# Per-head scale-and-add on VectorE in a gMLP and dilated-attention trunk: the merge of attention groups 0 and 1, and the output tiles

## The chip, the cores and the metric

The kernel runs on one core of a Trainium2 chip. The metric is the device time of one launch in microseconds (us). Names of engines: PE is TensorE, DVE is VectorE, ACT is ScalarE, POOL is GpSimd, SP is SyncE, which issues all the DMAs here.

## The reference

A trunk of two layers works on 2048 tokens of width 1024, all in float32. The first layer is a gated MLP with causal mixing inside chunks of 128 tokens. The second is attention in three groups of eight query heads of 128 columns each, with dilations 1, 4 and 16, over one shared K/V. What the change touches is how the three groups' results become one:

```
m = jnp.max(sc, axis=-1, keepdims=True)
p = jnp.exp(sc - m)
l = jnp.sum(p, axis=-1, keepdims=True)
...
lse = jnp.moveaxis((m + jnp.log(l))[..., 0], -1, 3)
...
alpha = jax.nn.softmax(jnp.stack(lses), axis=0)
o = jnp.sum(alpha[..., None] * jnp.stack(outs), axis=0).astype(x.dtype)
y = o.reshape(bsz, s, B_WIDTH) * jax.nn.silu(z)
return x + gate * (y @ w_out)
```

So for each token and head, three vectors of 128 columns are added with three weights, which differ by token and by head; the sum is multiplied by silu(z) and goes into the last matrix product.

## The kernel before

The tokens are worked through in four quarters of 512. For each quarter `layer_A` makes the gated MLP (products `v`, `u`, `z`, `o`), and `proj_B` makes K/V, the queries and z of the second layer. Every matrix is split into a high and a low part (`split`, lines 247 and 248: ACT copies the high part, DVE subtracts the low part), and a product is three passes on PE. The weights stream through a pool of 8 split buffers (`wp`) and 6 raw ones (`rp`).

Attention is a generator, `attend`, whose steps are called as side work ("fillers") between the matmuls of the main products by `tick`. A unit is one group `g`, one block `b` of 128 queries and one K/V head `kh` (four query heads). `att_1` transposes K and Q, `att_2` makes scores, maxima and exponentials (line 1103 on DVE adds distance times slope to the scores, line 1113 on ACT takes the exponentials), `att_3` transposes the probabilities (line 1155) and `att_4` multiplies them with V into the PSUM tile `po` (line 1174) and evacuates that into `ot`, which a DMA stores. Group 1 of quarter Q is worked off, and then group 0, beside `layer_A` of quarter Q + 1. The last quarter has no next one: its group 1 and group 0 run beside the output product.

**The merge of groups 0 and 1** sits in `att_3` and `att_4` for g = 0. `att_3` makes the factor `e1` for four heads (line 1134, ACT) and loads group 1's stored result `o1` (line 1136, a tile named `st_o`). `att_4` scales `o1` by `e1` on POOL (`scale_heads`, line 1225, one instruction over 128x512 with the factor broadcast along each head), updates the sums of weights on DVE with two instructions on 128x4 (lines 1169 and 1170), and adds `po` and the scaled `o1` on DVE (line 1178). There are 32 such units, 8 for each quarter.

**The output tiles** are in `finish`. For each of 16 tiles of 128 tokens, `load(t)` brings the merged result of groups 0 and 1 (`og[0]`), that of group 2 (`og[2]`) and z; `prepare(t)` scales `og[0]` by eight ACT instructions, one for each head (line 1287), scales `og[2]` on DVE (`scale_heads`, line 1225, 128x1024), adds the two on DVE (line 1289) and multiplies with z on POOL (line 1290). `make_yb(t)` transposes the result on PE (line 1312) and splits it (lines 1314 and 1315), and lines 1352 to 1354 are the output product `pf`, 48 matmuls for each tile, followed by line 1357 (DVE, gate), line 1358 (POOL, plus x) and a store. Tiles are prepared two ahead of the product. Tile 0 is prepared inside the last projection (`z3b`), tiles 1 to 11 beside group 1 of the last quarter, and the four tiles that need the last quarter's merge after it.

The order on each engine is not the order of the code alone: a scheduling pass sorts the instructions of all engines by its own costs, and each engine then works its list strictly in order. So an instruction that waits holds up everything behind it on its engine.

## Time and profile before

| | us |
|---|---|
| median of 3 runs | 2974.0 (2972.69 to 2979.12) |
| the profiled execution | 2975.72, of which its span is 2973.7 |
| PE busy | 2922.2 (98%) |
| DVE busy | 2114.8 (71%) |
| ACT busy | 1652.1 (56%) |
| POOL busy | 751.2 (25%) |

The page of the profile gives each engine's busy time, the span in 40 slices, and groups of instructions by line, each with its count, its busy time, the mean duration, and the idle time of its engine just ahead of it with the one that ended that idle time. The trace can also be asked for the busy times in a stretch of the span, for who waited for whom, and for single instructions in order of time. A busy PE is not PE at its peak, since the matmuls overlap: 512 columns are recorded as some 0.39 us, and the next one starts 0.23 us after.

### The profile page before, as it was taken

Reading aid. Unit: us, or ns where it says so; the run is one execution under the profiler, and the core shown is the slowest. Engines: PE = TensorE matmul, PEld = TensorE weight load, DVE = VectorE, ACT = ScalarE, POOL = GpSimd, SP = SyncE. Lnnn points to the kernel's source line nnn. Section 1 sums busy time; section 2 is a strip of 40 time slices with the busy share of each in tenths; the row PEclk is TensorE's granted clock in tenths of the full one; section 3 lists DMA queues with packets and bytes.
Section 4 is the critical chain, followed back from the end, with each engine's and each line's share of the span. In section 5 each row is a group of like instructions: output and inputs, shape, how many; then the busy total and the mean of one; then the engine's idle time right before and its main releaser. Section 6 shows DMA issues by size and latency. Waiting matters only on the chain. (4 is left out here: it accounts for less than half of the span.)

```text
span 2973.7 us, 45555 instructions
## 1 busy us (share of the span) xinstructions
PE 2922.2 (98%) x14752; PEld 2446.6 (82%) x14752; DVE 2114.8 (71%) x3794; ACT 1652.1 (56%) x3386; POOL 751.2 (25%) x1044
## 2 busy tenths in 40 slices
PE   7999999999999999999999999999999999999999
PEld 5888788878888888888888888888888888977887
DVE  6877676788556676877758676877668667878772
ACT  4323355766565365776546366675555457867440
POOL 1057002320002313502315214403314220122322
PEclk9999999999999999999999999999999999999999
DMA  8899975886344466884334466873333476788642
GB/s 280 275 306 341 310 237 179 261 301 203 123 125 125 131 196 203 280 271 128 110 115 132 139 196 210 298 243 107 115 117 122 137 228 193 230 285 289 221 162 92
DMA packets 368450, 596.08 MB, mean 200 GB/s; under 512 B 39018, under 2 KB 138572, under 8 KB 368212
## 3 DMA queue, kind: packets, MB, share of 16 engines
q1 hardware_dynamic: 368212, 593.17, 61.8%
q8 instruction: 117, 1.92, 0.3%
q14 instruction: 121, 0.99, 0.1%
HBM read 472.84 MB, written 120.20 MB: 199 GB/s over the span
## 5 line engine op out<-in xcount | busy, mean ns | idle before, releaser
L276 PE MATMUL pd_o<-w_o,yh 128*128 128x512 f32 x1024 | 324.8, 397 | 3.0 <-DVE w_o L248 3.0
L276 PE MATMUL pd_kv<-w_kv,hkh 128*128 128x512 f32 x768 | 239.3, 393 | 0.3
L276 PEld LDWEIGHTS pd_o<-w_o,yh 128*128 128x128 f32 x1024 | 187.7, 189 | 40.8 <-DVE w_o L248 4.2
L314 PE MATMUL pd_u<-hAh,w_u 128*128 128x512 f32 x512 | 208.0, 406 | 0.0
L314 PE MATMUL pd_z<-hAh,w_z 128*128 128x512 f32 x512 | 203.8, 398 | 0.0
L276 PE MATMUL pd_o<-w_o,yl 128*128 128x512 f32 x512 | 200.9, 393 | 0.0
L316 PE MATMUL pd_u<-hAh,w_u 128*128 128x512 f32 x512 | 200.6, 392 | 0.0
L316 PE MATMUL pd_z<-hAh,w_z 128*128 128x512 f32 x512 | 200.1, 391 | 0.0
L315 PE MATMUL pd_u<-hAl,w_u 128*128 128x512 f32 x512 | 199.7, 390 | 0.0
L315 PE MATMUL pd_z<-hAl,w_z 128*128 128x512 f32 x512 | 199.4, 389 | 0.0
L247 ACT ACTIVATE w_u<-raw_u 128x512 fp32r<-128x512 f32 x128 | 79.8, 629 | 166.9 <-PE pd_u L316 93.0
L247 ACT ACTIVATE w_z<-raw_z 128x512 fp32r<-128x512 f32 x128 | 80.3, 631 | 160.0 <-PE pd_z L316 74.5
L276 PEld LDWEIGHTS pd_kv<-w_kv,hkh 128*128 128x128 f32 x768 | 143.2, 189 | 30.7 <-ACT hkh L566 2.0
L248 DVE TENSOR_TENSOR w_z<-raw_z,w_z 128x512 fp32r<-128x512 f32 x128 | 108.2, 853 | 80.9 <-ACT w_z L247 80.4
L1174 PEld LDWEIGHTS po<-kv,pT 128*128 128x128 f32 x1200 | 148.1, 191 | 9.1 <-ACT pT L1019 2.2
L1174 PE MATMUL po<-kv,pT 128*128 128x128 f32 x1200 | 150.6, 275 | 1.2 <-ACT pT L1019 1.2
L247 ACT ACTIVATE w_o<-raw_o 128x512 fp32r<-128x512 f32 x128 | 79.4, 628 | 129.9 <-PE pd_o L276 92.2
L276 PE MATMUL pd_kv<-w_kv,hkl 128*128 128x512 f32 x384 | 149.5, 391 | 0.0
L1113 ACT ACTIVATE pr<-pr,stat,rt 128x256 f32<-128x256 f32 (+1 forms) x224 | 123.0, 551 | 31.1 <-DVE stat L1107 15.5
L248 DVE TENSOR_TENSOR w_o<-raw_o,w_o 128x512 fp32r<-128x512 f32 x128 | 94.7, 749 | 39.5 <-ACT w_o L247 38.2
L248 DVE TENSOR_TENSOR w_u<-raw_u,w_u 128x512 fp32r<-128x512 f32 x128 | 94.0, 749 | 34.0 <-ACT w_u L247 32.1
L248 DVE TENSOR_TENSOR w_q<-raw_q,w_q 128x512 fp32r<-128x512 f32 x144 | 96.9, 693 | 24.0 <-ACT w_q L247 22.9
(826 smaller groups left out, 8030.3 us busy)
## 6 DMA issues: line engine op xcount, KB each, us to landing
raw_q<-in_b_w_in_dram SPq DMA_DIRECT2D x144, 256.0 KB, 3.6
raw_u<-in_a_w_in_dram SPq DMA_DIRECT2D x128, 256.0 KB, 3.7
raw_z<-in_a_w_in_dram SPq DMA_DIRECT2D x128, 256.0 KB, 2.9
raw_o<-in_a_w_out_dram SPq DMA_DIRECT2D x128, 256.0 KB, 3.1
qt<-qd SPq DMA_DIRECT2D x96, 260.0 KB, 3.1
raw_v<-in_a_w_in_dram SPq DMA_DIRECT2D x96, 256.0 KB, 4.2
raw_kv<-in_w_kv_dram SPq DMA_DIRECT2D x96, 256.0 KB, 2.9
od<-ot SPq DMA_DIRECT2D x96, 256.0 KB, 2.7
```

The lines of the kernel that those rows point to most:

```text
L247: nc.scalar.activation(hi, src, AF.Copy)
L248: nc.vector.tensor_tensor(lo, src, hi.bitcast(F32), ALU.subtract)
L276: last_mm[0] = nc.tensor.matmul(pt, a, u[:, w, :], start=f, stop=e, skip_group_check=more)
L314: nc.tensor.matmul(pts[i], wh, hh[:, k, :], start=k == 0, stop=False)
L315: nc.tensor.matmul(pts[i], wh, hl[:, k, :], start=False, stop=False)
L316: nc.tensor.matmul(pts[i], wl, hh[:, k, :], start=False, stop=k == KT - 1)
L1113: nc.scalar.activation(pr[:, i, :], pr[:, i, :], AF.Exp, bias=mneg[:, i:i + 1], scale=u["rt"][:, h:h + 1], accum_out=lsum[:, i:i + 1])
L1174: nc.tensor.matmul(po[:, h * P:(h + 1) * P], u["pT"][h // hp][:, h % hp, j, :], u["kv"][:, j, kh, 1, :], start=j == 0, stop=j == nk - 1)
```

## The change

Two places change, and the helper `scale_heads` goes.

```
-            scale_heads(nc.gpsimd, u["o1"], u["o1"], e1)
             nc.vector.tensor_tensor(l1, l1, e1, ALU.mult)
             nc.vector.tensor_tensor(l0, l0, l1, ALU.add)
...
         if g == 0:
-            nc.vector.tensor_tensor(ot, po, u["o1"], ALU.add)
+            for h in range(4):
+                hs = slice(h * P, (h + 1) * P)
+                nc.vector.scalar_tensor_tensor(ot[:, hs], u["o1"][:, hs], stat[1][:, b, kh * 4 + h:kh * 4 + h + 1],
+                                               po[:, hs], ALU.mult, ALU.add)
...
-            scale_heads(nc.vector, og[2], og[2], st2[:, t, 0:8])
-            nc.vector.tensor_tensor(y, y, og[2], ALU.add)
+            for h in range(8):
+                hs = slice(h * P, (h + 1) * P)
+                nc.vector.scalar_tensor_tensor(y[:, hs], og[2][:, hs], st2[:, t, h:h + 1], y[:, hs],
+                                               ALU.mult, ALU.add)
```

In the merge, one POOL instruction and one DVE instruction on 128x512 become four DVE instructions on 128x128, each of which takes a head of `o1` times its factor plus that head of `po`. In an output tile, two DVE instructions on 128x1024 become eight on 128x128. The bytes moved by DMA and the matmuls stay what they were, in number and shape.

The scheduling pass gives other lists. PE's list is unchanged up to the start of the output product; from there on some steps of attention stand up to three `pf` matmuls earlier (the first one of the transposes `pp1_12_00` comes after 37 of them, where it came after 40). Three places show what moves elsewhere. The names carry group, block and head: `ot0_9_0` is group 0, block 9, K/V head 0; in `og6_0` and `og6_2` the first number is the tile and the second the group.

DVE in the merge of a middle quarter (group 0, block 9), before and then in the change; `w_o30_...` are split weights of the main product, `stat0` and `stat1` the sums:

```order
L248 TENSOR_TENSOR w_o30_1_1_21842<-raw_o30_1_1_21843,w_o30_1_1_21842 128x512
L1178 TENSOR_TENSOR ot0_9_0_21730<-po0_9_0_21721,st_o19_0_21613 128x512
L1070 COPY rt0_11_1_21996<-qt0_11_1_21817 128x8
L1169 TENSOR_TENSOR stat1_194<-stat1_194 128x4
L1170 TENSOR_TENSOR stat0_193<-stat0_193,stat1_194 128x4
L248 TENSOR_TENSOR w_o30_1_2_21847<-raw_o30_1_2_21848,w_o30_1_2_21847 128x512
```

```order
L248 TENSOR_TENSOR w_o30_1_1_21880<-raw_o30_1_1_21881,w_o30_1_1_21880 128x512
L1179 TENSOR_SCALAR ot0_9_0_21765<-st_o19_0_21649,stat1_194,po0_9_0_21756 128x128 x4
L1168 TENSOR_TENSOR stat1_194<-stat1_194 128x4
L1169 TENSOR_TENSOR stat0_193<-stat0_193,stat1_194 128x4
L248 TENSOR_TENSOR w_o30_1_2_21885<-raw_o30_1_2_21886,w_o30_1_2_21885 128x512
```

The four new instructions stand where the one stood; only a small copy has moved out from between.

DVE beside group 1 of the last quarter, where tile 6 is prepared, before and then in the change:

```order
L1225 TENSOR_TENSOR og6_2_27046<-og6_2_27046,wst_192 128x1024
L1106 TENSOR_REDUCE rt1_14_0_26743<-pr1_14_01_26840 128x2
L1066 TENSOR_SCALAR qT1_14_1_26869<-pq1_14_1_26864,gqk_481,qT1_14_1_26869 128x512
L1107 TENSOR_SCALAR stat1_194<-rt1_14_0_26743 128x2
L1017 COPY ot1_13_1_26886<-po1_13_1_26877 128x512
L1357 TENSOR_TENSOR of1_1_26892<-pf1_1_26754,gb1_25848 128x512
L1070 COPY rt1_15_1_27095<-qt1_15_1_26953 128x8
L1289 TENSOR_TENSOR og6_0_27044<-og6_0_27044,og6_2_27046 128x1024
L1017 COPY pT1_14_01_26914<-pp1_14_01_26909 128x512
```

```order
L1286 TENSOR_SCALAR og6_0_27122<-og6_2_27124,wst_192,og6_0_27122 128x128
L1106 TENSOR_REDUCE rt1_14_0_26809<-pr1_14_01_26912 128x2
L1066 TENSOR_SCALAR qT1_14_1_26941<-pq1_14_1_26936,gqk_481,qT1_14_1_26941 128x512
L1107 TENSOR_SCALAR stat1_194<-rt1_14_0_26809 128x2
L1286 TENSOR_SCALAR og6_0_27122<-og6_2_27124,wst_192,og6_0_27122 128x128 x3
L1017 COPY ot1_13_1_26958<-po1_13_1_26949 128x512
L1286 TENSOR_SCALAR og6_0_27122<-og6_2_27124,wst_192,og6_0_27122 128x128
L1355 TENSOR_TENSOR of1_1_26964<-pf1_1_26820,gb1_25896 128x512
L1070 COPY rt1_15_1_27173<-qt1_15_1_27025 128x8
L1286 TENSOR_SCALAR og6_0_27122<-og6_2_27124,wst_192,og6_0_27122 128x128 x3
L1017 COPY pT1_14_01_26986<-pp1_14_01_26981 128x512
```

The two long instructions become eight short ones, spread between the same steps of attention.

The last place is where group 0 of the last quarter begins, at block 12 beside output tile 5. ACT before, and then in the change:

```order
L1287 ACTIVATE og10_0_27992<-og10_0_27992,stat0_193 128x128 x7
L1287 ACTIVATE og11_0_28257<-og11_0_28257,stat0_193 128x128 x7
L1055 ACTIVATE kT0_12_27337<-pk0_12_27332 128x512
L1065 ACTIVATE qT0_12_0_27345<-pq0_12_0_27340,gqk_481 128x512
L1287 ACTIVATE og11_0_28257<-og11_0_28257,stat0_193 128x128
L1314 ACTIVATE yb5_27393<-pyb5_0_27394 128x512
```

```order
L1283 ACTIVATE og10_0_28102<-og10_0_28102,stat0_193 128x128 x8
L1055 ACTIVATE kT0_12_27421<-pk0_12_27416 128x512
L1065 ACTIVATE qT0_12_0_27429<-pq0_12_0_27424,gqk_481 128x512
L1312 ACTIVATE yb5_27477<-pyb5_0_27478 128x512
L1312 ACTIVATE yb5_27477<-pyb5_1_27485 128x512
L1283 ACTIVATE og11_0_28379<-og11_0_28379,stat0_193 128x128 x3
L1113 ACTIVATE pr0_12_00_27441,stat0_193<-pr0_12_00_27441,stat0_193,rt0_12_0_27432 128x256 x2
```

Seven scalings of tile 11 stood ahead of the two copies `kT0_12` and `qT0_12_0`; now none does, and three of them stand ahead of the exponentials `pr0_12_00`.

SP at the same place, before and then in the change:

```order
L1280 DMA zt10_27996<-zd_101 128x1024
L1278 DMA og11_0_28257<-od0_95 128x1024
L1339 DMA xr14_0_27303<-x1d_90 128x512
L1359 DMA out_0_dram<-of3_1_27299 128x512
L1136 DMA st_o112_1_27562<-od1_96 128x512
```

```order
L1357 DMA out_0_dram<-of3_1_27383 128x512
L1136 DMA st_o113_1_27903<-od1_96 128x512
L1136 DMA st_o114_0_28008<-od1_96 128x512
L1136 DMA st_o114_1_28159<-od1_96 128x512
L1136 DMA st_o115_0_28259<-od1_96 128x512
L1039 DMA qt0_13_0_27524<-qd0_92 128x520
L1274 DMA og11_0_28379<-od0_95 128x1024
L1357 DMA out_0_dram<-of4_0_27470 128x512
```

The load of tile 11 (`og11_0`) has moved from ahead of the store `of3_1` to behind the load of the queries `qt0_13_0`.

More of the change, by code (lines that the diff above doesn't have):

```diff
@@ L1219, in attend @@
                     yield
-    def scale_heads(e, out, t, f):
-        n = f.shape[-1]
-        e.tensor_tensor(out.rearrange("p (h d) -> p h d", d=P), t.rearrange("p (h d) -> p h d", d=P),
-                        f.unsqueeze(2).broadcast_to([P, n, P]), ALU.mult)
     sw = wst.rearrange("p (a g) (t c) -> p a (g t) c", a=4, c=16)
```

## The prediction

> **What bounds the kernel now.** First I read the span and the busy times of the engines, then the busy times by stage for the stages that the change touches.

> ```profile
> span 2973.7 us, 45555 instructions
> PE 2922.2 (98%) x14752; PEld 2446.6 (82%) x14752; DVE 2114.8 (71%) x3794; ACT 1652.1 (56%) x3386; POOL 751.2 (25%) x1044
> ```

> ```profile
> 905.00:1035.00 130.00, 129.35 (x699) 110.00 (x699) 94.32 (x203) 62.50 (x143) 43.59 (x56) 1.00 0.43 134
> 1560.00:1690.00 130.00, 130.00 (x708) 111.16 (x707) 95.26 (x204) 65.30 (x142) 56.78 (x72) 1.00 0.42 130
> 2205.00:2335.00 130.00, 130.00 (x712) 111.18 (x711) 101.53 (x216) 68.02 (x146) 56.90 (x72) 1.00 0.42 129
> 2690.00:2800.00 110.00, 101.55 (x633) 88.08 (x632) 85.39 (x152) 70.36 (x196) 37.96 (x19) 0.98 0.82 278
> 2800.00:2880.00 80.00, 79.92 (x517) 70.44 (x516) 67.78 (x155) 38.66 (x113) 20.96 (x17) 1.00 0.42 137
> ```

> Columns: the stage, its length, then busy us of PE, weight loads, DVE, ACT and POOL, the granted PE clock, DMA share and GB/s. The first three rows hold 24 of the 32 merges, the fifth the last 8. In these four PE stands still for 0.65, 0, 0 and 0.08 us. The fourth row, group 1 of the last quarter with ten output tiles, is the only stage touched that has idle PE time to speak of: 110 − 101.55 = 8.45 us.

> So I looked for who ends PE's idle time in the fourth stage, in the PE rows of the timeline (the four that the change can reach); the bracket has the idle time and its releaser.

> ```profile
> 2705.52 0.44 PE L1155 MATMUL pp<-ident,pr 128*128 128x128 f32 x2 [1.44 <-ACT pr L1113]
> 2742.51 0.44 PE L1155 MATMUL pp<-ident,pr 128*128 128x128 f32 x2 [1.21 <-ACT pr L1113]
> 2763.70 1.02 PE L1155 MATMUL pp<-ident,pr 128*128 128x128 f32 x4 [1.19 <-ACT pr L1113]
> 2793.18 0.58 PE L1098 MATMUL ps<-kT,qT 128*128 128x256 f32 x1 [2.90 <-ACT qT L1065]
> ```

> Three waits are for the exponentials of a unit (together 3.84 us), one of 2.90 us is for a copy of transposed queries. Nearly everything else is PE's own time.

> **The merges.** Removed per unit: one POOL scaling and one DVE add. Added: four DVE instructions on 128x128.

> ```profile
> L1225 POOL TENSOR_TENSOR st_o<-st_o,stat x32: 1032/1042/1530, 925.1 to 2866.7; 128x512 f32<-128x512 f32 x32
> L1178 DVE TENSOR_TENSOR ot<-po,st_o 128x512 f32<-128x512 f32 x32 | 21.9, 684 | 13.2 <-PE po L1174 12.9 <-DMA raw_o<-in_a_w_out_dram 0.2
> L1103 DVE SCALAR_TENSOR_TENSOR b_s<-dist,rt,ps 128x128 f32<-128x128 f32 x64 | 18.0, 343 | 3.3 <-PE ps L1094 3.3
> ```

> The third row is the new instruction's twin: the same operation, 128x128, one operand in SBUF, one in PSUM, a factor per partition, 343 ns. Four are 4 x 343 = 1372 ns against 684, so DVE gets 688 ns more per unit: the fused form is not less DVE work, it pays a start four times. [...]

> Against it stands something that the removed POOL instruction does to DVE:

> ```profile
> L1169 DVE TENSOR_TENSOR stat<-stat 128x4 f32<-128x4 f32 x32 | 10.6, 332 | 6.2 <-ACT stat L1134 6.2
> L1170 DVE TENSOR_TENSOR stat<-stat,stat x32: 145/388/1228, 919.2 to 2867.8; 128x4 f32<-128x4 f32 x32
> L1170 DVE TENSOR_TENSOR stat<-stat,stat 128x4 f32<-128x4 f32 x32 | 15.6, 487 | 0.7
> L1169 DVE TENSOR_TENSOR stat<-stat x32: 145/164/996, 919.0 to 2866.8; 128x4 f32<-128x4 f32 x32
> ```

> Two instructions on 128x4 that can run in 145 to 164 ns take 332 and 487 ns on average and up to 1228, about the length of a POOL scaling that starts on the same event. If all of that excess is POOL holding DVE up, a unit gets back (332 − 164) + (487 − 164) = 491 ns. So DVE's net is between +197 and +688 ns per unit, at most 8 x 688 = 5.5 us in a stage of 130 us in which DVE is idle for 28 us or more (101.53 of 130 in the fullest). On the path that costs nothing as long as PE is fed ahead:

> ```profile
> L247 ACT ACTIVATE w_o<-raw_o 128x512 fp32r<-128x512 f32 x128 | 79.4, 628 | 129.9 <-PE pd_o L276 92.2
> ```

> ACT, the first of the two that split weights, waits 92 us for PE to free a buffer; DVE follows ACT. Weights are ready up to 8 buffers ahead, so 0.7 us in a DVE queue is absorbed. If that cover failed, the 24 units of the first three stages could cost 24 x 0.688 = 16.5 us at the very most; idle PE time of 0 to 0.65 us says they don't. I take **0** for all 32 merges, with 0 to +2 us in the range.

> **The output tiles.** Removed per tile: two DVE instructions. Added: eight. Both operands lie in SBUF, for which the trace has no 128x128 row; the nearest is 128x512.

> ```profile
> L1225 DVE TENSOR_TENSOR og<-og,wst x16: 1210/1220/3086, 2650.3 to 2893.4; 128x1024 f32<-128x1024 f32 x16
> L1289 DVE TENSOR_TENSOR og<-og,og x16: 1212/1220/2570, 2654.1 to 2895.6; 128x1024 f32<-128x1024 f32 x16
> L709 DVE SCALAR_TENSOR_TENSOR acc_a<-aw,sc,acc_a 128x512 f32<-128x512 f32 x28 | 21.0, 751 | 0.8
> L838 DVE SCALAR_TENSOR_TENSOR mt<-pm,colsb,b_s 128x512 f32<-128x512 f32 x64 | 47.4, 744 | 11.0 <-PE pm L836 10.2
> ```

> At 512 columns the operation takes 751 ns from SBUF and 744 with one operand in PSUM, so I take the 343 ns again: 8 x 343 = 2744 ns against 1220 + 1220 = 2440, **+0.30 us a tile**. The ends: a quarter of 751 is 188 ns each, which makes −0.94 us a tile; and one full hold-up by POOL in each tile, of the length that the longest row shows (3086 − 1220 = 1.87 us), makes +2.17. For the ten tiles of the fourth stage that is +3.0 us of DVE (−9.4 to +21.7) where DVE is idle for 110 − 85.4 = 24.6 us. What of it is on the path: the three waits for exponentials are units without cover, and DVE's scores and maxima stand ahead of the exponentials. At about a tile a unit I charge each wait 0.30 us, so +0.9, and 0.2 for the first, whose transposes come three matmuls (0.7 us) earlier while its scores come two earlier (0.5 us). **+1.1 us.** The eight pieces let an urgent step pass sooner than a piece of 1.22 us did; that would cut into the same three waits, and is priced among the rivals. Tile 0, in the last projection, ends within half a microsecond of where it did, since its last add waits for ACT either way: 0. The six tiles left lie beside a PE that is idle for 0.08 us: 0.

> **The wait of 2.90 us.** This is where the new lists matter most.

> ```profile
> 2698.53 0.28 PE L1098 MATMUL ps<-kT,qT 128*128 128x256 f32 x1
> 2698.65 0.28 PE L1099 MATMUL ps<-kT,qT 128*128 128x256 f32 x1
> ...
> 2783.41 0.32 SPq L1278 DMA_DIRECT2D og<-od  x1
> 2784.02 0.39 PE L1353 MATMUL pf<-wo,yb 128*128 128x512 f32 x1
> 2784.24 0.39 PE L1354 MATMUL pf<-wo,yb 128*128 128x512 f32 x1
> 2787.88 0.60 PE L1050 MATMUL pk<-ident,kv 128*128 128x128 f32 x4
> 2788.31 0.60 PE L1060 MATMUL pq<-ident,qt 128*128 128x128 f32 x4
> 2788.94 0.32 SPq L1039 DMA_DIRECT2D qt<-qd  x1
> 2789.92 2.15 ACT L1287 ACTIVATE og<-og,stat 128x128 f32<-128x128 f32 x7 [10.06 <-DMA og<-od]
> 2791.98 0.58 ACT L1055 ACTIVATE kT<-pk 128x512 fp32r<-128x512 f32 x1
> 2792.46 0.67 ACT L1065 ACTIVATE qT<-pq,gqk 128x512 fp32r<-128x512 f32 x1
> ```

> The first two rows give the pace of score matmuls (0.12 us), the two of `pf` that of the product (0.22 to 0.23), and the two of four transposes each begin 0.43 apart. PE had K and Q transposed by 2788.9, but ACT stood idle for 10.06 us on the load of tile 11, whose scalings were ahead of the two copies. In the new list none of tile 11 is ahead of them: kT and qT are done by about 2788.5 + 0.58 + 0.67 = 2789.8, before PE gets there at 2790.3, and the 2.90 us go. What is late next: tile 11's load now follows the query load, so it goes out at about 2789.3 and not at 2783.4, and three scalings of tile 11 stand ahead of the exponentials.

> ```profile
> DMA to landing us min/median/max: 3.8/4.9/6.6
> ```

> This load takes 4.9 us (3.8 to 6.6), so it lands at 2794.2 (2793.1 to 2795.9). Three scalings at 2.15/7 = 0.31 us each and one exponential of 0.6 us later, the first transposes may start at 2795.7 (2794.6 to 2797.4). PE comes there at about 2795.3: from 2790.3, twelve score matmuls at 0.12, twelve transposes at 0.43/4 and ten product matmuls at 0.23 make 5.0. So a wait of about 0.5 us (0 to 2.1) takes the place of 2.90.

> A second part hangs on it, the clock:

> ```profile
> 2700.00:2720.00 20.00, 18.30 (x123) 15.79 (x123) 19.14 (x35) 18.92 (x53) 5.90 (x3) 1.00 0.82 292
> ...
> 2792.00:2794.00 2.00, 0.82 (x4) 0.82 (x4) 1.41 (x3) 1.42 (x4) 0.00 (x0) 0.78 1.02 387
> 2794.00:2796.00 2.00, 2.00 (x11) 2.00 (x11) 1.03 (x3) 0.00 (x0) 1.27 (x1) 0.50 0.25 94
> 2796.00:2798.00 2.00, 2.00 (x13) 1.85 (x13) 2.00 (x6) 1.09 (x2) 0.00 (x0) 0.87 0.55 192
> ```

> Right behind the wait the granted clock falls to 0.50; the last three rows lose 2 x (0.22 + 0.50 + 0.13) = 1.7 us of PE. Around the wait of 1.44 us at 2705, in the first row, it stays at 1.00. So with a wait of 0.5 us I expect the clock to stay. [...]

> Term: −(2.90 − 0.5) − 1.7 = **−4.1 us** (0 if the wait only moves, −4.6 if nothing takes its place).

> **The sum**, against the profiled execution of 2975.72 us (span 2973.7): merges 0, tiles +1.1, wait and clock −4.1, together −3.0, so 2972.7. That execution lies 1.7 us above the median of 2974.0, and the prediction for the median is **2971.0 us**.

> **Rivals.**
> *POOL holds up the pieces (slower).* Each of the eight pieces reads two SBUF operands, as did the long ones that took up to 3086 ns, and POOL has a product of 2.4 us for each tile:

> ```profile
> L1290 POOL TENSOR_TENSOR og<-og,zt x16: 2377/2395/3167, 2655.5 to 2898.8; 128x1024 f32<-128x1024 f32 x16
> ```

> If each tile meets one hold-up of 1.87 us with a unit's scores behind it, DVE gets 21.7 us where 24.6 are idle and becomes the bound there: the three uncovered waits grow by 3 x 2.17 = 6.5, two of them pass 2.9 us and take the clock down (2 x 1.7), and the gain at tile 11 is lost: 2974.0 + 9.9 = **2984**. For it: the maximum of 3086. Against it: the medians are 1220. It decides from a mean of some 550 ns for the new instruction.
> *Finer pieces free the exponentials (faster).* The waits of 3.84 us vanish as well as the 4.6 us at tile 11: 2974.0 − 8.4 = **2966**. For it: a piece blocks DVE for 0.34 us, not 1.22. Against it: more DVE time in sum, and the same count of ACT scalings.
> *The change does not do what it says.* It spares POOL 32 x 1.04 = 33 us and burdens DVE with up to 32 x 0.69 + 16 x 0.30 = 27 us, and neither engine is the bound; if the wait at tile 11 only moves behind the exponentials with its clock fall, nothing is left but +1.1: **2975**.

> **How the numbers follow.** A measurement of this kernel can tell about 0.2% (6 us) from no change, so the line is at 2968 and 2980. My forecast has a chance of 0.48 and the third rival 0.18, both within 0.2%; the faster rival 0.16, the slower one 0.18. Hence faster 0.16, same 0.66, slower 0.18. The range: the terms' bounds give 2974.0 − 8.4 to 2974.0 + 9.9; I leave out the upper part of the slower rival: 2965 to 2982.

> **What would show it.** Right: the four new merge instructions at 340 to 350 ns each with no POOL beside them, lines 1168 and 1169 of the changed kernel back near 150 ns, PE idle of under 1 us in each of the three middle stages, no wait for qT near 2790 and no fall of the clock there, DVE busy up by 7 to 27 us with the span hardly moved. Wrong: a mean above 500 ns for line 1286, PE waits for exponentials over 2 us, or a new fall of the clock in the output stage; and any gap of PE in the middle stages, since I priced those at nothing.

## The result, and the profile after

The changed kernel takes **2979.33 us** (median of 22 runs, 2972.76 to 2988.11), the kernel before 2973.91 in the same series (22 runs). The ratio is 1.0018 [1.001, 1.0025]: 5.4 us slower, just inside what the prediction called no change, where 3 us faster was forecast. The profiled execution took 2978.11 us. Its page begins (first the span, then busy us of each engine):

```profile
span 2976.1 us, 45685 instructions
PE 2920.2 (98%) x14752; PEld 2444.2 (82%) x14752; DVE 2106.2 (71%) x3986; ACT 1651.7 (55%) x3386; POOL 712.8 (24%) x1012
```

DVE has 192 instructions more and 8.6 us less than before. That difference is no effect of its own: a second profile of the kernel before has DVE busy for 2106.7 us. The same five stages as before (length, then busy us of PE, weight loads, DVE, ACT, POOL, granted clock, DMA share, GB/s):

```profile
905.00:1035.00 130.00, 129.48 (x701) 110.12 (x700) 93.93 (x227) 62.26 (x143) 34.70 (x48) 1.00 0.43 134
1560.00:1690.00 130.00, 130.00 (x709) 111.08 (x708) 95.44 (x227) 64.58 (x139) 47.71 (x64) 1.00 0.42 129
2205.00:2335.00 130.00, 130.00 (x710) 111.11 (x709) 98.91 (x241) 68.50 (x146) 47.26 (x64) 1.00 0.41 129
2690.00:2800.00 110.00, 100.84 (x632) 86.12 (x630) 87.36 (x210) 66.97 (x186) 35.53 (x19) 1.00 0.82 272
2800.00:2880.00 80.00, 78.41 (x512) 69.63 (x512) 65.59 (x194) 41.92 (x122) 12.74 (x8) 1.00 0.44 142
```

In the three merge stages PE still stands idle for half a microsecond or none. The clock stays at 1.00 where it had been 0.98, and yet the fourth stage has more idle PE time than before, 9.2 us. The new instructions, by line (nanoseconds least, median, most; where; shape):

```profile
L1179 DVE SCALAR_TENSOR_TENSOR ot<-st_o,stat,po x128: 333/341/350, 938.0 to 2879.3; 128x128 f32<-128x128 f32 x128
L1286 DVE SCALAR_TENSOR_TENSOR og<-og,wst,og x128: 335/344/2479, 2651.9 to 2897.6; 128x128 f32<-128x128 f32 x128
```

The pieces of the merges (L1179, one operand in PSUM) never take more than 350 ns. Those of the output tiles (L1286, both operands in SBUF) have the same median and a longest of 2479. Here is that one in the timeline of the changed kernel, and 25 us later another (start, length, engine, line, what; the bracket is the idle time before and who ended it):

```profile
2723.78 2.74 DVE L1286 SCALAR_TENSOR_TENSOR og<-og,wst,og 128x128 f32<-128x128 f32 x2
2723.93 2.44 POOL L1288 TENSOR_TENSOR og<-og,zt 128x1024 f32<-128x1024 f32 x1 [6.63 <-DMA kv<-kvd]
...
2726.44 1.25 DVE L1103 SCALAR_TENSOR_TENSOR pr<-dist,rt,ps 128x256 f32<-128x256 f32 x3
...
2727.45 0.63 PE L1310 MATMUL pyb<-ident,og 128*128 128x128 f32 x4 [0.73 <-DVE pr L1103]
...
2728.84 0.60 ACT L1113 ACTIVATE pr<-pr,stat,rt 128x256 f32<-128x256 f32 x1 [2.63 <-DVE stat L1107]
...
2748.32 2.38 POOL L1288 TENSOR_TENSOR og<-og,zt 128x1024 f32<-128x1024 f32 x1 [1.31 <-DVE og L1286]
...
2748.70 2.67 DVE L1286 SCALAR_TENSOR_TENSOR og<-og,wst,og 128x128 f32<-128x128 f32 x3
...
2751.29 1.25 DVE L1103 SCALAR_TENSOR_TENSOR pr<-dist,rt,ps 128x256 f32<-128x256 f32 x3
...
2752.20 2.05 PE L1173 MATMUL po<-kv,pT 128*128 128x128 f32 x16 [0.76 <-DVE pr L1103]
...
2753.69 0.60 ACT L1113 ACTIVATE pr<-pr,stat,rt 128x256 f32<-128x256 f32 x1 [3.46 <-DVE stat L1107]
```

POOL multiplies a finished tile by z (L1288, 2.4 us) from the moment its last piece is done. In DVE's new list the next tile's pieces stand right behind that last piece. One of them begins beside POOL's product and ends some 0.15 us after it: 2.1 to 2.5 us for a piece of 0.34. Behind them in DVE's queue wait the scores of a unit (L1103). PE waits for those, and ACT stands idle for 2.63 and 3.46 us until its exponentials have their maxima. A third such piece, of 2115 ns, lies at 2735.33. A fourth, at 2876, has of attention only the last merge behind it, and PE loses nothing there: from tile 6 to the last matmul of the product both kernels take 137.0 us.

The wait of the exponentials for their maxima between 2690 and 2770, in the changed kernel and then in the kernel before (a second profile of it), in total us, times, longest:

```profile
ACT pr L1113 <- DVE stat L1107: 10.0, 6, 3.5
```

```profile
ACT pr L1113 <- DVE stat L1107: 4.7, 4, 2.6
```

The other profile of each kernel has 10.5 and 4.5 us. PE's own waits for the exponentials do not tell the kernels apart: 4.3 and 2.2 us in the two profiles of the changed kernel, 3.8 and 2.1 in those of the kernel before.

For the rest, one table goes by the product with the output weights (`pf`, 48 matmuls a tile). **Tiles 0-2** is the time from the start of tile 0's first matmul to that of tile 3's; the expectations call it the first 144. **Tiles 3-5** goes on to tile 6's. The ratio is that of a kernel's runs to runs of before on the same chip. PE's idle time in tiles 0-2 is 8.0 and 8.5 us in the two profiles of the changed kernel, and 4.3 and 3.6 before.

| kernel | tiles 0-2 | tiles 3-5 | median | ratio, interval |
|---|---|---|---|---|
| before, first and second profile | 75.0, 74.2 | 63.8, 62.9 | 2973.91 | |
| changed, first and second profile | 80.4, 82.5 | 60.4, 62.2 | 2979.33, 2979.95 | 1.0018 [1.001, 1.0025], 1.0018 [1.0006, 1.0029] |
| merges only | 74.8 | 61.7 | 2974.67 | 1.0004 [0.9996, 1.0013] |
| tiles only | 81.0 | 60.9 | 2977.26 | 1.0013 [1.0005, 1.0022] |
| changed, product in pieces | 77.2 | 61.3 | 2975.54 | 1.0009 [0.9999, 1.0019] |
| before, product in pieces | 80.0 | 62.4 | 2976.70 | 1.0014 [1.0005, 1.0022] |
| changed, one column of the product | 74.4 | 60.3 | 2969.47 | 0.9982 [0.9973, 0.9991] |
| before, one column of the product | 73.9 | 62.9 | 2973.84 | 1.0001 [0.9992, 1.001] |
| changed, product on DVE | 75.3 | 64.1 | 2973.53 | 0.9994 [0.9984, 1.0004] |
| changed, one operand in PSUM | 70.6 | 59.5 | 2964.01 | 0.997 [0.9957, 0.9982] |
| before, sum from PSUM | 71.9 | 61.4 | 2970.75 | 0.9993 [0.9983, 1.0003] |
| changed, held back only | 73.9 | 66.0 | 2978.06 | 1.0014 [1.0005, 1.0023] |

### The profile page after: what moved, and what is told of

Same layout as the page of the kernel before. It is cut to its first block, busy times and chain, and to the rows that moved or that the text cites. A ratio compares the mean times of both kernels' runs of the same rounds, so it can differ in the third digit from the quotient of the medians.

```text
span 2976.1 us, 45685 instructions
## 1 busy us (share of the span) xinstructions
PE 2920.2 (98%) x14752; PEld 2444.2 (82%) x14752; DVE 2106.2 (71%) x3986; ACT 1651.7 (55%) x3386; POOL 712.8 (24%) x1012
## 4 chain that ended last, share of the span: by engine, by line
PE 76%; DMA 9%; DVE 6%; issue 4%; ACT 2%; POOL 2%; SPq 1%; POOLq 0%; DVEq 0%; ACTq 0%
PE pd_o L276 11%; PE pd_kv L276 7%; PE po L1173 4%; PE pd_u L314 3%; PE pd_u L316 3%; PE pd_z L316 3%; PE pd_z L314 3%; PE pd_u L315 3%; PE pd_z L315 3%; PE pm L836 1%; PE pd_v1b L276 1%; PE pd_v2b L276 1%; PE pd_v2a L276 1%; DMA raw_z<-in_a_w_in_dram 1%; PE pq L1060 1%
## 5 line engine op out<-in xcount | busy, mean ns | idle before, releaser
L276 PE MATMUL pd_o<-w_o,yh 128*128 128x512 f32 x1024 | 323.5, 396 | 1.6 <-DVE w_o L248 1.6
L276 PE MATMUL pd_kv<-w_kv,hkh 128*128 128x512 f32 x768 | 239.0, 393 | 0.3
L276 PEld LDWEIGHTS pd_o<-w_o,yh 128*128 128x128 f32 x1024 | 187.0, 188 | 39.0 <-DVE w_o L248 2.9
L276 PE MATMUL pd_o<-w_o,yl 128*128 128x512 f32 x512 | 200.2, 392 | 0.0
L247 ACT ACTIVATE w_u<-raw_u 128x512 fp32r<-128x512 f32 x128 | 79.8, 629 | 165.3 <-PE pd_u L316 96.0
L247 ACT ACTIVATE w_z<-raw_z 128x512 fp32r<-128x512 f32 x128 | 80.3, 631 | 159.2 <-PE pd_z L316 74.5
L276 PEld LDWEIGHTS pd_kv<-w_kv,hkh 128*128 128x128 f32 x768 | 143.0, 188 | 30.6 <-ACT hkh L566 2.0
L247 ACT ACTIVATE w_o<-raw_o 128x512 fp32r<-128x512 f32 x128 | 79.5, 628 | 140.1 <-PE pd_o L276 83.2
L1173 PEld LDWEIGHTS po<-kv,pT 128*128 128x128 f32 x1200 | 148.0, 191 | 10.2 <-ACT pT L1019 1.6
L276 PE MATMUL pd_kv<-w_kv,hkl 128*128 128x512 f32 x384 | 149.6, 391 | 0.0
L1113 ACT ACTIVATE pr<-pr,stat,rt 128x256 f32<-128x256 f32 (+1 forms) x224 | 123.0, 551 | 32.7 <-DVE stat L1107 24.4
L1121 POOL TENSOR_TENSOR dg<-pr,ident 128x256 f32<-128x256 f32 x38 | 30.0, 789 | 417.3 <-DVE stat L1168 209.5
```

Of the source, the lines that this page charges most:

```text
L247: nc.scalar.activation(hi, src, AF.Copy)
L276: last_mm[0] = nc.tensor.matmul(pt, a, u[:, w, :], start=f, stop=e, skip_group_check=more)
L1113: nc.scalar.activation(pr[:, i, :], pr[:, i, :], AF.Exp, bias=mneg[:, i:i + 1], scale=u["rt"][:, h:h + 1], accum_out=lsum[:, i:i + 1])
L1121: nc.gpsimd.tensor_tensor(dg, prev, ident.unsqueeze(1).broadcast_to([P, hp, P]), ALU.mult)
L1173: nc.tensor.matmul(po[:, h * P:(h + 1) * P], u["pT"][h // hp][:, h % hp, j, :], u["kv"][:, j, kh, 1, :], start=j == 0, stop=j == nk - 1)
```

## The experiments

The theory (A): POOL's long product holds up the pieces of the next tile, and attention behind them pays. The rivals: the new lists themselves cost the time (B), the pieces' own DVE time does (D), or the merges do (M).

**One part alone.** First the merges without the tiles: in the changed kernel

```diff
-            for h in range(8):
-                hs = slice(h * P, (h + 1) * P)
-                nc.vector.scalar_tensor_tensor(y[:, hs], og[2][:, hs], st2[:, t, h:h + 1], y[:, hs],
-                                               ALU.mult, ALU.add)
+            scale_heads(nc.vector, og[2], og[2], st2[:, t, 0:8])
+            nc.vector.tensor_tensor(y, y, og[2], ALU.add)
```

> Only the merge part of the change, the output tiles as before. PE's list is that of before but for the order of two rows. Theory A (POOL's product of 2.4 us holds up the short pieces of the output tiles, and attention steps wait behind them), theory B (the new lists of the output stage cost it) and theory D (the pieces' own DVE time costs it) all put the whole loss in the tiles: within 2 us of before, PE idle under 1 us in each of the three middle stages, the waits for exponentials in the output stage at 3 to 4 us as before, and the wait of 2.9 us for qT near 2790 still there. Rival M (the merges cost the time): +4 to +6 us against before.

Then the opposite: the same edit reversed, in the kernel before.

> Only the output tiles of the change, the merges as before. PE's list is word for word that of the changed kernel. A, B and D: the whole loss is here, +3 to +6 us against before, about +5 between the first and the 144th matmul of the output projection, -3 to -4 between the 144th and the 240th, waits for exponentials of about 10 us. Rival M: within 1 us of before.

The merges alone are not to be told from before (1.0004), with 74.8 us for tiles 0-2 and 0.54, 0 and 0 us of idle PE in the merge stages. The tiles alone take 81.0 us there, and show the same pieces of 2474, 2112 and 2146 ns at the same places. M falls. One miss: the merges alone kept the wait for qT, but it was 1.34 us and not 2.9, without a fall of the clock. So the wait is not the same in every execution, which matters below.

**POOL's product in pieces.** In the changed kernel, and as a control in the one before, only POOL's list differs:

```diff
-            nc.gpsimd.tensor_tensor(y, y, og["z"], ALU.mult)
+            for h in range(8):
+                hs = slice(h * P, (h + 1) * P)
+                nc.gpsimd.tensor_tensor(y[:, hs], y[:, hs], og["z"][:, hs], ALU.mult)
```

> The changed kernel with POOL's product with z in eight pieces of 128x128 in place of one of 128x1024; the lists of PE, ACT and DVE are word for word those of the changed kernel, only POOL's differs. A: no piece is held up for longer than a short POOL piece lasts, so the longest of the pieces falls from 2479 ns to below 900, the waits of ACT's exponentials for DVE's maxima fall from 10 us to 2 to 4, and the time falls by 3 to 6 us against the changed kernel, to 2973 to 2976 or below. B and D: neither the lists nor the count of pieces are different, so the time stays within 1 us of the changed kernel, +4 to +6 against before.

> The kernel before with the same product in eight pieces, the control to the run above; the lists of PE, ACT and DVE are those of before. A: here DVE's long pieces are held up too (longest 3086 and 2570 ns, together some 1.8 us over eight tiles), but little urgent stands behind them: 0 to 2 us faster than before, the wait of 2.9 us at tile 11 still there. B and D: within 1 us of before. If the split itself costs something (a POOL piece with a fixed start), both this run and the one above show it alike.

The group of the pieces between 2690 and 2770 (busy us, mean ns), in the changed kernel and then in the one with the split; and the latter's wait of the exponentials there:

```profile
L1286 DVE SCALAR_TENSOR_TENSOR og<-og,wst,og 128x128 f32<-128x128 f32 x64 | 24.6, 433 | 2.5 <-ACT yb L1312 2.5
```

```profile
L1286 DVE SCALAR_TENSOR_TENSOR og<-og,wst,og 128x128 f32<-128x128 f32 x64 | 23.4, 412 | 2.1 <-DMA og<-od 2.1
```

```profile
ACT pr L1113 <- DVE stat L1107: 4.6, 5, 1.6
```

The mean is hardly lower, but now DVE's pieces alternate with POOL's and take about 545 ns each there, and none there is held longer than 596 ns. The waits for maxima fall from 10.0 to 4.6 us and tiles 0-2 from 80.4 to 77.2, over half of the way to before's 75.0. With nearly the same sum, shorter blocks cost less. On the whole time the gain is less than A expected: 1.0009 against 1.0018 is some 2.7 us, not 3 to 6. And the control did not come out as expected: before with the same split was slower, 80.0 us. Its trace shows where: a wait of 3.12 us for exponentials at 2741, and around its end 6.8 us at half the clock, worth 3.4 us (same columns as the stages). Why those exponentials came so late stays open.

```profile
2741.65 0.69 PE L1155 MATMUL pp<-ident,pr 128*128 128x128 f32 x2 [3.12 <-ACT pr L1113]
```

```profile
2740.00:2742.00 2.00, 0.35 (x3) 0.35 (x3) 0.00 (x0) 2.00 (x8) 0.63 (x1) 0.68 0.88 281
2742.00:2744.00 2.00, 2.00 (x8) 1.66 (x7) 1.82 (x3) 1.54 (x6) 0.29 (x1) 0.50 0.85 228
```

So splitting has effects of its own, and this pair cannot give A's full price.

**The product left out but for one column of each head.** This takes the hold-up away and leaves the lists of PE, ACT and DVE word for word, in both kernels (here `v` stands for `rearrange("p (h d) -> p h d", d=P)[:, :, 0:1]`):

```diff
-            nc.gpsimd.tensor_tensor(y, y, og["z"], ALU.mult)
+            nc.gpsimd.tensor_tensor(v(y), v(y), v(og["z"]), ALU.mult)
```

> The changed kernel, but POOL multiplies only one column of each head with z (128x8 in place of 128x1024), so the rest of the product is left out; the lists of PE, ACT and DVE are word for word those of the changed kernel. From the first to the 144th matmul of the output projection, the changed kernel took 80.4 us, the tiles alone 81.0, the kernel before 75.0, the merges alone 74.8, and the changed kernel with the product in eight pieces 77.2. A (POOL's long product holds up the pieces, which causes all of the loss): 75 to 76 us, no piece longer than 450 ns, waits of the exponentials for DVE's maxima below 4 us, and in the end 3 to 6 us faster than the changed kernel. B (the new lists themselves, or the eight pieces' own DVE time): the 77.2 us of the split product stay, 77 to 78 us, and 2 us faster than the changed kernel at most.

> The kernel before with the same part of POOL's product left out, the control: lists of PE, ACT and DVE as before. One scaling was held up to 3086 ns here. A: the stretch takes 74 to 75 us (75.0 before), the difference between this run and the one above is 1 us or less there, and the time is 0 to 2 us below before. B: as here, and the one above stays 2 to 3 us longer in this stretch.

The pieces of the changed kernel, the same window:

```profile
L1286 DVE SCALAR_TENSOR_TENSOR og<-og,wst,og 128x128 f32<-128x128 f32 x72 | 21.3, 344 | 1.3 <-DMA og<-od 1.3
```

This pair decides. Without the product, tiles 0-2 take 74.4 us with the change and 73.9 without it: the new lists and the eight pieces cost **0.5 us** (one profile of each), so B and D fall. With the product they take 80.4 to 82.5 and 74.2 to 75.0. The hold-up costs the changed kernel **6.0 to 8.0 us** and the one before 0.3 to 1.1; 1.7 of the 8.0 are a clock fall in the second profile. Without the hold-up the change is faster than before, 0.9982 [0.9973, 0.9991], while the kernel before gains nothing on the whole from the same edit (1.0001). From 1.0018 to 0.9982 are 10.7 us, more than the traces show in tiles 0-2; the rest is not located. One of A's expectations, no piece above 450 ns, was not met: a piece of 1400 ns begins at 2870.57. POOL's other instruction of an output tile, the addition of x, runs beside it and ends just before it:

```profile
2870.31 1.92 DVE L1286 SCALAR_TENSOR_TENSOR og<-og,wst,og 128x128 f32<-128x128 f32 x3
...
2870.53 1.29 POOL L1357 TENSOR_TENSOR of<-of,xr 128x512 f32<-128x512 f32 x1 [1.99 <-DVE of L1356]
```

So this is the same hold-up by a shorter instruction. It is there in the changed kernel (1394 ns) and with the split (1386) too.

**The product on DVE**, nothing left out:

```diff
-            nc.gpsimd.tensor_tensor(y, y, og["z"], ALU.mult)
+            nc.vector.tensor_tensor(y, y, og["z"], ALU.mult)
```

> The changed kernel with the product with z on DVE in place of POOL; nothing is left out. POOL holds nothing up in a tile, and DVE gets 1.2 us more a tile (a sum of 128x1024 took 1.22 us), 10 to 12 us of the 24 us in which it is idle in the stage with ten tiles. The lists are made anew and differ in some places. A: the three hold-ups of 2.1 to 2.5 us go, which pays for half of the added DVE time: the stretch takes 76 to 79 us, between the changed kernel and before. B or D (DVE's own time is what counts): 81 to 84 us, slower than the changed kernel by 1 to 4 us.

75.3 us for tiles 0-2, better than A itself expected: 1.22 us more DVE work per tile costs less than being held up three times. Tiles 3-5 take 64.1, and this version ends level with before (0.9994). Each of its two stretches holds a clock fall worth 1.7 us.

**One operand in PSUM.** The pieces of the merges were never held up. For tiles 2 to 15 this gives the output pieces the same form:

```diff
+            pw = [pst(f"pw{t}_{n}", "d") for n in range(2)] if t > 1 else [y[:, 0:512], y[:, 512:1024]]
             for h in range(8):
-                nc.scalar.activation(y[:, hs], y[:, hs], AF.Copy, scale=stat[0][:, t, h:h + 1])
+                nc.scalar.activation(pw[h // 4][:, hp], y[:, hs], AF.Copy, scale=stat[0][:, t, h:h + 1])
             for h in range(8):
-                nc.vector.scalar_tensor_tensor(y[:, hs], og[2][:, hs], st2[:, t, h:h + 1], y[:, hs],
+                nc.vector.scalar_tensor_tensor(y[:, hs], og[2][:, hs], st2[:, t, h:h + 1], pw[h // 4][:, hp],
                                                ALU.mult, ALU.add)
```

(`hp` is head h's place in its half.) The two kernels were run again beside it:

> The changed kernel, with the scaled part of group 0 written by ACT into PSUM for tiles 2 to 15, so that each piece reads one operand from SBUF and one from PSUM; POOL's product of 2.4 us stays whole and nothing is left out. The lists are made anew and differ in some places. A, in the form that POOL holds up a DVE instruction only where both its operands lie in SBUF (the 60 pieces of the merges with POOL beside them, one operand in PSUM, took 349 ns at most): no piece above 450 ns although POOL's product runs beside some, 74 to 76 us from the first to the 144th matmul of the output projection, and 3 to 6 us faster than the changed kernel, at or below the kernel before. Rival (POOL holds up any DVE instruction that touches its data or its turn): pieces of 2 us and more as before, 78 to 81 us. Where the two PSUM buffers per tile are scarce, PE waits for a buffer of the product, which would be seen at its first matmuls.

> The kernel before once more, for a second profile. From the 1st to the 144th matmul of the output projection 74.8 to 75.2 us as in the first profile and in the run of the merges alone. From the 144th to the 288th the first profile had 63.8 and the merges alone, with the same PE list, 61.7: if the wait of 2.90 us with its clock fall is what the kernel always has, 63.8 again; if it varies, 61 to 63 and no clock fall.

> The changed kernel once more, for a second profile and a second ratio: 80 to 81 us from the 1st to the 144th matmul with the same three pieces of 2.1 to 2.5 us, 60.4 to 60.9 from the 144th to the 288th, and 3 to 7 us slower than before.

The pieces with an operand in PSUM; then what POOL does to others in the same run; then the fourth stage, the one with ten output tiles:

```profile
L1287 DVE SCALAR_TENSOR_TENSOR og<-og,wst,pw x112: 335/340/349, 2700.6 to 2927.0; 128x128 f32<-128x128 f32 x112
```

```profile
2724.20 2.40 POOL L1289 TENSOR_TENSOR og<-og,zt 128x1024 f32<-128x1024 f32 x1 [8.36 <-DVE og L1287]
...
2724.61 0.69 DVE L1056 TENSOR_TENSOR kT<-pk,kT 128x512 fp32r<-128x512 f32 x1
...
2725.22 1.40 DVE L1107 SCALAR_TENSOR_TENSOR stat<-rt 128x2 f32<-128x2 f32 x1
```

```profile
2690.00:2800.00 110.00, 108.78 (x696) 95.54 (x695) 83.12 (x205) 64.22 (x178) 25.87 (x15) 1.00 0.75 250
```

None of the 112 pieces is above 349 ns, though 43 ran beside a POOL instruction for over 30% of their time. In the second view, beside POOL's product, the subtraction that reads PSUM (`pk`) takes its 0.69 us, while a 128x2 operation in SBUF takes 1.40 us and ends with the product, at 2726.6; at 2723.65, ahead of the product, the same line took 0.15 us. The longest piece with both operands in SBUF took 2479 ns (in the changed kernel), the longest of these 112 with one in PSUM 349.

PE's idle time in the fourth stage falls to 1.2 us, and this kernel **beats both**: 2964.01 us, 0.997 [0.9957, 0.9982] to before. It is more than A expected (70.6 us against 74 to 76), so something else helps as well. The second profiles repeat the picture, though three of their stretches miss the expected values. Before has 74.2 (74.8 to 75.2 were expected) and 62.9, its wait for qT now 2.11 us without a fall of the clock. The changed kernel has 82.5 and 62.2 (80 to 81 and 60.4 to 60.9), with its three pieces of 2473, 2109 and 2155 ns; each of its stretches holds a clock fall worth 1.7 us, and without it both would be as expected.

**What else the PSUM version does.** Two PSUM buffers per tile also hold the tiles back: POOL reached the product of tile 7 at 2812 us there, and at 2757 in the changed kernel. So work moves out of the stage with the most attention (theory P). Two runs separate this. One gives PSUM to the kernel before, with the sum in halves:

```diff
             scale_heads(nc.vector, og[2], og[2], st2[:, t, 0:8])
-            nc.vector.tensor_tensor(y, y, og[2], ALU.add)
+            for n in range(2):
+                ns = slice(n * 512, (n + 1) * 512)
+                nc.vector.tensor_tensor(y[:, ns], pw[n], og[2][:, ns], ALU.add)
```

> The kernel before with the scaled part of group 0 written into PSUM for tiles 2 to 15, the sum in two halves of 128x512 that read it from there, and the scaling of group 2 on DVE as before, both operands in SBUF; nothing is left out. In the changed kernel the same edit took the first 144 matmuls of the output projection from 80.4 and 82.5 to 70.6 us. Theory A (no hold-up is all of that gain): here few hold-ups were there to lose, about 1.1 us, so 73 to 75 us (75.0 and 74.2 before), and the time 0 to 3 us below before. Theory P (the PSUM buffers also hold the tiles back, so that less of DVE's and ACT's work lies in the stage with attention): 70 to 72 us, and 8 to 12 us faster than before.

The other holds the tiles back in the changed kernel, while the pieces stay in SBUF:

```diff
+            for p in pw:
+                nc.scalar.activation(p[:, 0:1], y[:, 0:1], AF.Copy)
             ...
+            for p in pw:
+                nc.vector.tensor_copy(og[2][:, 0:1], p[:, 0:1])
```

> The changed kernel with the same two PSUM buffers held per tile, touched in one column only (two short copies on ACT and two on DVE more a tile), while the pieces read both operands from SBUF as in the change; nothing is left out. Theory P (holding the tiles back is the gain): 70 to 73 us for the first 144 matmuls and 2963 to 2967 us. Theory A (only the operand in PSUM saves the pieces from POOL): pieces of 2 us and more stay, 78 to 82 us, and 2976 to 2980 us. Both in part: few such pieces, since the next tile no longer stands right behind POOL's product, and 73 to 77 us.

Held back, the kernel before does tiles 0-2 in 71.9 us, and the changed one in 73.9 with one hold-up left, of 2179 ns at 2723.98. So holding back is worth some 2 to 3 us there for the kernel before, and P holds for that stretch. P's times do not follow: the two end at 0.9993 and 1.0014, and in the second the later tiles pay (66.0 us for tiles 3-5, of which a clock fall is 1.7). In the PSUM version both things help: its fused pieces need 130.0 us for tiles 0-5, and the long instructions with PSUM 133.3, with a scaling of 3091 ns among them. Of its gain over before, 11 us between the medians and 9 by the ratio, the traces show 8 in tiles 0-5 (130.0 against 138.0, the mean of before's two profiles); the rest is not located.

## Why the prediction was wrong

**The merges (0): right.** PE's idle time in their stages and the run of the merges alone (1.0004) agree. Their DVE price was too high, though. By groups (busy us, mean ns of one):

```profile
L1179 DVE SCALAR_TENSOR_TENSOR ot<-st_o,stat,po 128x128 f32<-128x128 f32 x128 | 35.9, 340 | 15.0 <-PE po L1173 14.2 <-DMA qt<-qd 0.6 <-issue 0.2
```

```profile
L1168 DVE TENSOR_TENSOR stat<-stat 128x4 f32<-128x4 f32 x32 | 9.1, 285 | 4.6 <-ACT stat L1134 4.6
L1169 DVE TENSOR_TENSOR stat<-stat,stat 128x4 f32<-128x4 f32 x32 | 8.6, 269 | 0.5
```

A piece lasts 340 ns, as forecast (343), but 35.9 / 128 = 280 ns of busy time falls to each, since one begins before the last has ended. So a unit's four cost 1122 ns and not 1372, +438 instead of +688. The short instructions did not go back to 150 ns: they got (332 − 285) + (487 − 269) = 265 ns, of 491. POOL's scaling was only part of what held them up. In the middle stages those of over 250 ns end with other POOL instructions, of 0.4 to 1.3 us. Net +173 ns a unit, just below the range of +197 to +688, and no PE time. DVE's total was forecast to rise by 7 to 27 us, and it fell by 8.6 from the first profile of before and by 0.5 from the second. Merges, their short instructions and tiles come to +8.6 us together, so 9 to 17 us came back in other DVE instructions. The run of the merges alone shows the same: DVE is busy for 2099.6 us there, 7 to 15 less than before, though its merges and their short instructions add about 5. That POOL's scaling had held up these instructions too fits this, but which ones, and how much, differs between executions.

**The output tiles (+1.1): the step that failed.** The eight pieces themselves and the new lists cost 0.5 us, so the charge of 0.30 us for each wait was, if anything, too much. What was left out of the sum is the hold-up. It stood in the prediction as the rival *POOL holds up the pieces*, with a chance of 0.18, and was set aside because the medians of the long instructions were 1220 ns. That was the wrong evidence. What counts here is what stands in DVE's list when POOL's product begins. In the kernel before, two of these places look like this (its second profile):

```profile
2706.33 2.39 POOL L1290 TENSOR_TENSOR og<-og,zt 128x1024 f32<-128x1024 f32 x1 [5.71 <-DVE og L1289]
...
2706.72 3.09 DVE L1225 TENSOR_TENSOR og<-og,wst 128x1024 f32<-128x1024 f32 x1
...
2746.36 2.39 POOL L1290 TENSOR_TENSOR og<-og,zt 128x1024 f32<-128x1024 f32 x1 [2.50 <-DMA out_dram<-of]
...
2746.65 1.25 DVE L1103 SCALAR_TENSOR_TENSOR pr<-dist,rt,ps 128x256 f32<-128x256 f32 x3
...
2748.88 1.22 DVE L1225 TENSOR_TENSOR og<-og,wst 128x1024 f32<-128x1024 f32 x1
```

The first scaling ran into the product. Later ones began just after it, with scores from PSUM in between. In the new list pieces of the next tile follow at once, and the order of the changed kernel, known beforehand, could have shown it. The rival's price was too high (+9.9 us), and its "mean of some 550 ns" was no deciding point: 433 ns between 2690 and 2770 sufficed, because three pieces of over 2 us with scores behind them do the harm.

**The wait at tile 11 (−4.1): right in kind, too large.** No profile of the changed kernel waits for qT near 2790, and the load of tile 11 goes out behind that of the queries, as forecast. What takes its place, in the first profile:

```profile
2794.46 0.32 SPq L1039 DMA_DIRECT2D qt<-qd  x1
...
2794.88 0.38 SPq L1274 DMA_DIRECT2D og<-od  x1
...
2800.99 0.98 ACT L1283 ACTIVATE og<-og,stat 128x128 f32<-128x128 f32 x3 [2.04 <-DMA out_dram<-of]
...
2802.61 0.44 PE L1155 MATMUL pp<-ident,pr 128*128 128x128 f32 x2 [1.59 <-ACT pr L1113]
```

Three scalings, then the exponentials (the bracket names a store; that the scalings waited for tile 11's load is inferred from the order, since its landing is not recorded), and a wait of 1.59 us (1.88 in the second profile), within the bounds of 0 to 2.1 but not 0.5. The other half of the error is that one execution of the kernel before was taken for the rule. Its wait was 2.90 us with the clock fallen, then 2.11, and 1.34 for the merges alone, both with the clock at 1.00. Means over the three profiles without the tile part (63.8, 62.9, 61.7) and the three with it (60.4, 62.2, 60.9) give −1.7 us for tiles 3-5.

**The sum.** The same means give +6.6 us for tiles 0-2 (81.3 against 74.7), so +5.0 with tiles 3-5, beside +5.4 and +4.9 between the medians. Predicted for the two were +1.1 and −4.1. Of the other rivals, *Finer pieces free the exponentials* did not come about: with the hold-up taken away the median was 2969.5 us, near its 2966, but tiles 0-2, where its three waits lie, were no shorter with the pieces (74.4) than without (73.9). Half of *The change does not do what it says* did: in the second profile the wait at tile 11 only moved behind the exponentials and kept a clock fall. Its 2975 left the hold-up out as well.

## What to carry to other kernels

Before splitting or fusing DVE work whose operands both lie in SBUF, look at what POOL runs when those instructions come up in the list: here three pieces of 0.34 us beside a POOL instruction of 2.4 us took 2.1 to 2.5 us, and everything queued behind them paid. With an operand in PSUM none of the 128 pieces of the merges and of the 112 of the output tiles took more than 350 ns. A wait seen in one profile is a sample: price its removal from two or three.

## What the runs showed of the hardware

The clock did not follow the length of a wait. In the second profile of the changed kernel it fell behind waits of 1.95 and 1.88 us; with the product in pieces it stayed at 1.00 behind one of 2.57 us. For each kernel first the waits, then the windows (same columns as the stages):

```profile
2770.78 1.02 PE L1155 MATMUL pp<-ident,pr 128*128 128x128 f32 x4 [1.95 <-ACT pr L1113]
...
2805.96 0.44 PE L1155 MATMUL pp<-ident,pr 128*128 128x128 f32 x2 [1.88 <-ACT pr L1113]
```

```profile
2772.00:2774.00 2.00, 2.00 (x8) 1.57 (x7) 0.53 (x1) 1.54 (x5) 1.33 (x1) 0.53 0.91 339
...
2804.00:2806.00 2.00, 0.12 (x2) 0.04 (x1) 0.50 (x5) 1.66 (x6) 0.00 (x0) 1.00 0.98 301
2806.00:2808.00 2.00, 2.00 (x8) 1.61 (x9) 0.90 (x2) 2.00 (x6) 0.00 (x0) 0.57 1.01 373
```

```profile
2800.31 0.44 PE L1155 MATMUL pp<-ident,pr 128*128 128x128 f32 x2 [2.57 <-ACT pr L1113]
```

```profile
2798.00:2800.00 2.00, 0.00 (x0) 0.00 (x0) 0.16 (x1) 1.31 (x4) 0.00 (x0) 1.00 0.87 312
2800.00:2802.00 2.00, 1.69 (x10) 1.40 (x10) 0.55 (x1) 2.00 (x8) 0.00 (x0) 1.00 0.99 393
2802.00:2804.00 2.00, 2.00 (x18) 1.92 (x17) 2.00 (x8) 2.00 (x8) 0.70 (x2) 1.00 0.28 109
```
